# One stationary operand for two neighbouring chunks at all six dyadic levels of an HGRN2 head, the odd chunk's keys and values in reversed order

## The chip, the cores and the metric

The kernel runs on one core of a Trainium2 chip. The metric is the device time of one execution in microseconds (us), the median of several runs. Engines: PE (TensorE, matmuls), DVE (VectorE), ACT (ScalarE), POOL (GpSimd), and SP (SyncE), which issues most of the DMAs.

## What is computed

A decoder layer over 1024 tokens with 16 learned meta tokens ahead of them (D_MODEL 1024, float32): a norm, one input projection, an HGRN2 recurrence of four heads beside a pooling mixer, gates that merge the two, an output projection, and a gated MLP. The change lies in the recurrence:

```python
def _hgrn2_chunk_step(state, xs):
    q, k, v, lf = xs
    b = jnp.cumsum(lf, axis=2)
    o_inter = jnp.einsum('bhtk,bhkv->bhtv', q * jnp.exp(b), state)
    diff = b[:, :, :, None, :] - b[:, :, None, :, :]
    decay = jnp.where(causal, jnp.exp(jnp.where(causal, diff, 0.0)), 0.0)
    scores = jnp.einsum('bhtk,bhtsk,bhsk->bhts', q, decay, k)
    o_intra = jnp.einsum('bhts,bhsv->bhtv', scores, v)
    k_dec = k * jnp.exp(b_last[:, :, None, :] - b)
    new_state = jnp.exp(b_last)[..., None] * state + jnp.einsum('bhsk,bhsv->bhkv', k_dec, v)
    return new_state, o_inter + o_intra
```

The kernel works in chunks of 128 tokens, eight of them and one of the 16 meta tokens. Within a chunk the decay between query t and key s is not a product of one factor of t and one of s that stays in range, so the lower triangle of a chunk is cut into blocks: the pairs within two neighbours (the basic scores, `sb`), and for lv = 2, 4, ... 64 the squares in which the query lies in the second half and the key in the first half of a run of 2 lv tokens. In each such square the decay is taken from the middle of the run, and queries and keys each get a factor of their own.

## The kernel before

Until 250 us the kernel makes norms, the values v, which it stores to DRAM (`vscr`), and the first gates. Then comes the head stage, to about 510 us, and behind it the branch products, the output projection and the MLP. Matrix products are split by hand into a high and a low part (`whi`, `wlo`, `uhi`, `ulo`); the weights' split is a cast on ACT (L140) and a difference on DVE or POOL (L141).

In the head stage the list `ORDER` interleaves projections with the heads: `F` (forget gate, banks `pf`), `Q` (query, `pq`), `G` (output gate, `pg`), `PV` and others are projections, `h0` to `h3` take a head one step further, `c0` to `c3` run a head's logarithms. A list `POOLED` puts single vector operations on POOL; what isn't in it runs on DVE. Within that, the order of ACT's, DVE's and POOL's instructions is set by a scheduler when the program is built, and each engine takes its instructions strictly in that order. The steps of a head:

- `post_f` and `chain_f`: two sigmoids of the forget projection on ACT (f, and 1 - f as kk), three scalings (L600 to L602), two logarithms (L605, L606), their sum on DVE (L607) and the running sum b by a scan of nine parts (L609).
- `level_in`, for the pairs (2, 4), (8, 16), (32, 64): the difference of b to its middle (L643), two exponentials (L646, L647), then the query product (L648) and the key product (L649). Level 64 has no difference but sixteen small exponentials with a bias for each chunk (L640, L641), and a negated middle, `neg` (L638).
- `level_mm`: the matmuls into one bank `sl`. Levels 2 to 16 take a chunk's whole 128 columns of keys and queries as the stationary operand and the 64 queries as the moving one, eight matmuls (L664); what lies outside the squares is not used. Levels 32 and 64 take just the squares, sixteen of 32x32 and eight of 64x64 (L660). Levels 2 to 8 also have a small product of the meta tokens (`sm`, L669).
- `level_out`: a masked copy to the scores `sc` on DVE (L684), or copies on ACT for 32 and 64 (L678).
- then qs and kd, the exponentials of the recurrence (L700, L705), e1 for the basic scores (L715, L716, products L719, L720), transposes of kd (`pt`, copied to kt and ktm at L728 and L732), the basic scores (`sb`, L737, L738), the state products (`ds`, L749, L756) and the outputs (`po`).

The matmuls use eight PSUM banks in turn; one that writes to a bank waits until the engine that empties it is done.

## Time and profile before

| | |
|---|---|
| median of 3 runs | 1367.0 us (1366.5 to 1367.03) |
| profiled execution, span of the core | 1364.2 us, granted PE clock 0.998 |
| PE busy | 1334.8 us (98%) |
| DVE, ACT, POOL busy | 931.3, 601.7, 426.5 us |
| bytes moved by DMA | 236.67 MB, mean 173 GB/s |

The span runs from the first to the last instruction of the core; the median of the runs is 2.8 us above it. In rows of the profile the first two numbers are a start and a duration in us, then engine, line, operation, output tile, input tiles and shapes; "x16" counts instructions in a row, and what stands in brackets is the idle time ahead of it and what ended that. One fp32 matmul shows as two rows. Tile names are printed without their numbers.

### The profile page before, as it was taken

How to read it: one execution, taken by the hardware profiler on the slowest of the kernel's cores; microseconds unless marked ns; L12 is line 12 of the kernel's file. 1: busy time of each engine (PE TensorE's matmuls, PEld its weight loads, DVE VectorE, ACT ScalarE, POOL GpSimd, SP SyncE). 2: the span in 40 equal slices, each digit the busy share in tenths (PEclk: the TensorE clock that was granted, in tenths of full speed). 3: DMA queues.
4: the chain of work that ended last, by engine and by line, in shares of the span. 5: the costliest groups of instructions: out<-in, count | busy, mean ns of one | idle time of the engine just before them, and what ended most of it. 6: DMA issues, size and time to landing. Idle time of an engine off the chain costs nothing. (4 is left out here: it accounts for less than half of the span.)

```text
span 1364.2 us, 20180 instructions
## 1 busy us (share of the span) xinstructions
PE 1334.8 (98%) x7737; PEld 1183.7 (87%) x7737; DVE 931.3 (68%) x1242; ACT 601.7 (44%) x1066; POOL 426.5 (31%) x324
## 2 busy tenths in 40 slices
PE   8999999999989999999999999999999999999997
PEld 7799999999989999987778888888888887888786
DVE  6755644378756557666568888888878777644557
ACT  6543333479766574225655222222322223543343
POOL 2014421227233600051020555454557742000100
PEclk9999999999999999999999999999999999999999
DMA  7134433321110158988876877656677799965534
GB/s 265 48 117 140 124 114 104 101 63 32 49 34 18 34 183 291 323 252 300 286 266 237 230 207 201 193 177 165 158 164 170 181 235 271 380 204 190 183 95 154
DMA packets 141455, 236.67 MB, mean 173 GB/s; under 512 B 9255, under 2 KB 77451, under 8 KB 141359
## 3 DMA queue, kind: packets, MB, share of 16 engines
q1 hardware_dynamic: 129294, 211.00, 46.5%
q0 software_dynamic: 12064, 24.38, 10.5%
q8 instruction: 61, 1.00, 0.3%
q14 instruction: 36, 0.29, 0.1%
HBM read 171.85 MB, written 86.53 MB: 189 GB/s over the span
## 5 line engine op out<-in xcount | busy, mean ns | idle before, releaser
L287 PE MATMUL P<-v,whi 128*128 128x512 f32 (+2 forms) x408 | 142.0, 356 | 3.3 <-ACT p L1501 1.7
L288 PE MATMUL P<-v,whi 128*128 128x512 f32 (+2 forms) x408 | 141.2, 353 | 0.0
L290 PE MATMUL P<-v,wlo 128*128 128x512 f32 (+2 forms) x424 | 135.9, 351 | 0.0
L175 PE MATMUL pd<-rot 128*128 128x512 f32 x272 | 105.9, 390 | 0.3 <-DVE rot L1428 0.3
L176 PE MATMUL pd<-rot 128*128 128x512 f32 x272 | 105.8, 389 | 0.0
L141 POOL TENSOR_TENSOR wlo<-wraw,whi 128x1024 fp32r<-128x1024 f32 (+1 forms) x19 | 45.9, 2416 | 161.9 <-ACT whi L140 86.1
L1428 DVE TENSOR_TENSOR rot<-yt,rot 128x1024 fp32r<-128x1024 f32 x33 | 41.2, 1249 | 72.6 <-ACT rot L1427 72.6
L287 PEld LDWEIGHTS P<-v,whi 128*128 128x128 f32 x408 | 77.2, 189 | 14.5 <-ACT p L1501 2.1
L232 ACT CAST whi<-wraw 128x512 fp32r<-128x512 f32 x78 | 46.1, 618 | 98.0 <-PE P L288 78.8
L288 PEld LDWEIGHTS P<-v,whi 128*128 128x128 f32 x408 | 77.2, 189 | 10.6 <-issue 0.2
L290 PEld LDWEIGHTS P<-v,wlo 128*128 128x128 f32 x424 | 74.3, 189 | 11.4
L233 DVE TENSOR_TENSOR wlo<-wraw,whi 128x512 fp32r<-128x512 f32 x74 | 68.4, 946 | 20.1 <-ACT whi L232 20.1
L1316 POOL TENSOR_TENSOR ys<-y 128x512 f32<-128x512 f32 x22 | 35.3, 1603 | 135.5 <-DVE y L1374 51.5
L1427 ACT CAST rot<-yt 128x1024 fp32r<-128x1024 f32 x33 | 34.6, 1052 | 91.5 <-PE pd L175 91.5
L174 PE MATMUL pd<-rot 128*128 128x512 f32 x272 | 72.6, 390 | 2.1 <-ACT rot L1427 1.2
L258 POOL TENSOR_TENSOR swa<-wraw,wraw 128x512 f32<-128x512 f32 x28 | 44.5, 1591 | 92.9 <-DMA wraw<-in_w_in_dram 56.8
L232 ACT CAST whi<-swa 128x512 fp32r<-128x512 f32 x56 | 33.4, 619 | 86.1 <-PE P L288 77.5
L1360 DVE SCALAR_TENSOR_TENSOR y<-g,par,y 128x1024 f32<-128x1024 f32 x44 | 64.8, 1472 | 0.8
L140 ACT CAST whi<-wraw 128x1024 fp32r<-128x1024 f32 (+1 forms) x28 | 26.4, 942 | 85.4 <-PE ppv L188 17.2
L174 PEld LDWEIGHTS pd<-rot 128*128 128x128 f32 x272 | 51.0, 188 | 13.4 <-ACT rot L1427 1.6
L232 ACT CAST whi<-swb 128x512 fp32r<-128x512 f32 x56 | 33.4, 618 | 63.1 <-PE P L288 59.3
L175 PEld LDWEIGHTS pd<-rot 128*128 128x128 f32 x272 | 51.1, 188 | 11.3 <-DVE rot L1428 0.7
(391 smaller groups left out, 4191.2 us busy)
## 6 DMA issues: line engine op xcount, KB each, us to landing
wraw<-in_w_in_dram SPq DMA_DIRECT2D x36, 512.0 KB
yt<-ysum SPq DMA_DIRECT2D x33, 512.0 KB
wraw<-in_ffn_w_gate_dram SPq DMA_DIRECT2D x26, 512.0 KB
wraw<-in_w_out_dram SPq DMA_DIRECT2D x24, 512.0 KB
wraw<-in_ffn_w_up_dram SPq DMA_DIRECT2D x22, 512.0 KB
wsum<-in_ffn_w_down_dram SPq DMA_DIRECT2D x22, 512.0 KB
ysum<-ys SPq DMA_DIRECT2D x11, 768.0 KB
sa<-sscr SPq DMA_DIRECT2D x16, 513.0 KB
```

The costliest lines, as they stand in the source:

```text
L141: eng.tensor_tensor(lo, raw, rr(hi), ALU.subtract)
L174: pe.matmul(ps, ahi, bhi, start=first, stop=False)
L175: pe.matmul(ps, ahi, blo, start=False, stop=False)
L176: pe.matmul(ps, alo, bhi, start=False, stop=last)
L232: act.copy(hi, src)
L233: (pool_e if 4 <= i < 2 * self.early else dve).tensor_tensor(lo, src, rr(hi), ALU.subtract)
L258: pool_e.tensor_tensor(s1, a21, a22, ALU.add)
L287: pe.matmul(d, whi[:, k, :], xh[:, c : c + w], start=(k == 0 and onto is None), stop=False, **go)
L288: pe.matmul(d, whi[:, k, :], xl[:, c : c + w], start=False, stop=False, **go)
L290: pe.matmul(x[:, o : o + w], wlo[:, k, :], xh[:, c : c + w], start=False, stop=(k == 3), **go)
L1360: dve.scalar_tensor_tensor(a, g[:, j : j + SEQ], cvw[:, j, m : m + 1], a, ALU.mult, ALU.add)
L1428: dve.tensor_tensor(lo, src, rr(hi), ALU.subtract)
```

## The change

Two neighbouring chunks now have one stationary operand. Of each chunk only the keys of first halves are used at a level, 64 of 128 columns. The odd chunk's keys are stored in reversed order, and then its first halves fall, seen from the chunk's end, on the columns that the even chunk leaves free. So the key products of an even and an odd chunk are written into the two halves of one 128-column operand in a new tile `dk`, and one matmul multiplies it with the 128 queries of both chunks. A level takes four matmuls of 128x128 instead of eight, and levels 32 and 64 have the same form.

What goes with it: the second sigmoid is written to b, and kk is scaled from there in three pieces, the odd chunks' reversed (L613, L615); every key product is done in two halves, with a piece of its own for the meta tokens on levels 2 to 8 (L666, L670); e1's key product in three (L737, L741); the copies of levels 32 and 64 to sc become six per head instead of three (L693); kd's exponentials of odd chunks write reversed (L721). The masks become twice as wide, and those of 32 and 64 go. The values of odd chunks are needed reversed as well: four DMAs copy a stored chunk from DRAM to DRAM in reversed order (L516), each behind the store of that chunk on SP, and each head loads its values by two DMAs instead of one. The program has 7211 matmul instructions for 7339, 945 DVE tensor_tensor instructions for 909, 36 ACT table loads for 32, and 386 ACT activations for 378.

The core of the diff:

```diff
-            nc.sync.dma_start(vd[(t0 - NM) // P], v)
+            c = (t0 - NM) // P
+            nc.sync.dma_start(vd[c % 2, c // 2], v)
+            if c % 2:
+                there, here = (vd[i, c // 2].rearrange("t (j v) -> j t v", j=2) for i in (2, 1))
+                nc.sync.dma_start(there, here[:, ::-1])
...
-            act.activation(kk[:, lo : lo + n], ps[:, :n], AF.Sigmoid, scale=-1.0)
+            act.activation(b[:, lo : lo + n], ps[:, :n], AF.Sigmoid, scale=-1.0)
...
-        act.activation(kk, kk, AF.Copy, scale=oml[:, hh])
+        act.activation(kk[:, :NM], b[:, :NM], AF.Copy, scale=oml[:, hh])
+        for z in range(2):
+            act.activation(parity(kk, z), time_order(b, z), AF.Copy, scale=oml[:, hh])
...
+    def parity(t, z):
+        return t[:, NM:L].rearrange("p (c z t) -> p c z t", z=2, t=P)[:, :, z, :]
+
+    def time_order(t, z):
+        return parity(t, z)[:, :, ::-1] if z else parity(t, z)
...
-            eng(f"lk{lv}.{h}").tensor_tensor(db[:, :, 0, :], db[:, :, 0, :], blocks(kk, lo, lv)[:, :, 0, :], ALU.mult)
-            return d
-
-        def level_mm(lv, qk):
+            e = eng(f"lk{lv}.{h}")
+            if lo == 0:
+                dm, km = (t[:, :NM].rearrange("p (b two h) -> p b two h", two=2, h=lv)[:, :, 0, :] for t in (d, kk))
+                e.tensor_tensor(dm, dm, km, ALU.mult)
+            for z in range(2):
+                o_, a, b_ = (t.rearrange("p c (b two h) -> p c b two h", two=2, h=lv)[:, :, :, z, :]
+                             for t in (dk.rearrange("p (c t) -> p c t", t=P), time_order(d, z), parity(kk, z)))
+                e.tensor_tensor(o_, a, b_, ALU.mult)
+            return d, dk
+
+        def level_mm(lv, qk, dk):
             ps = bank("sl")
-            half = lv >= 32
-            for c in range(NCH):
-                t = NM + c * P
-                if half:
-                    for i in range(P // (2 * lv)):
-                        s, n = t + 2 * lv * i, 2 * lv * i
-                        pe.matmul(ps[n : n + lv, c * lv : (c + 1) * lv], qk[:, s : s + lv], qk[:, s + lv : s + 2 * lv],
-                                  start=True, stop=True)
-                    continue
-                rhs = qk[:, t : t + P].rearrange("p (b two h) -> p b two h", two=2, h=lv)[:, :, 1, :]
-                pe.matmul(ps[:, c * 64 : (c + 1) * 64], qk[:, t : t + P], rhs, start=True, stop=True)
+            for c in range(NCH // 2):
+                t = NM + 2 * c * P
+                rhs = qk[:, t : t + 2 * P].rearrange("p (b two h) -> p b two h", two=2, h=lv)[:, :, 1, :]
+                pe.matmul(ps[:, c * P : (c + 1) * P], dk[:, c * P : (c + 1) * P], rhs, start=True, stop=True)
...
-                o3 = sc.rearrange("p (c t) -> p c t", c=NCH)
-                p3 = ps[:, : NCH * lv].rearrange("p (c h) -> p c h", c=NCH)
+                o4 = sc.rearrange("p (c z t) -> p c z t", z=2, t=P)
+                p4 = ps.rearrange("p (c z t) -> p c z t", z=2, t=P // 2)
                 for i in range(P // (2 * lv)):
-                    n = 2 * lv * i
-                    act.copy(o3[n : n + lv, :, n + lv : n + 2 * lv], p3[n : n + lv])
+                    q0 = 2 * lv * i + lv
+                    for z, n in ((0, 2 * lv * i), (1, P - 2 * lv * i - lv)):
+                        act.copy(o4[n : n + lv, :, z, q0 : q0 + lv], p4[n : n + lv, :, z, lv * i : lv * (i + 1)])
...
-                act.activation(kc[:, c], bc[:, c], AF.Exp, bias=bc[:, c, w - 1 : w], scale=-1.0)
+                kt_ = kc[:, c, ::-1] if t0 and c % 2 else kc[:, c]
+                act.activation(kt_, bc[:, c], AF.Exp, bias=bc[:, c, w - 1 : w], scale=-1.0)
...
-        k2 = kk.rearrange("p (b two) -> p b two", two=2)[:, :, 1]
         eng(f"e1q.{h}").tensor_tensor(q2, q2, e1[:, : L // 2], ALU.mult)
-        eng(f"e1k.{h}").tensor_tensor(k2, k2, e1[:, L // 2 :], ALU.mult)
+        ek = e1[:, L // 2 :]
+        km = kk[:, :NM].rearrange("p (b two) -> p b two", two=2)[:, :, 1]
+        eng(f"e1k.{h}").tensor_tensor(km, km, ek[:, : NM // 2], ALU.mult)
+        ek = ek[:, NM // 2 :].rearrange("p (c z t) -> p c z t", z=2, t=P // 2)
+        for z in range(2):
+            k2 = parity(kk, z).rearrange("p c (b two) -> p c b two", two=2)[:, :, :, 1 - z]
+            eng(f"e1k.{h}").tensor_tensor(k2, k2, ek[:, :, z, ::-1] if z else ek[:, :, z], ALU.mult)
```

Lines move by 11 to 21: what was L605 and L606 is L618 and L619, L609 is L622, L638 L652, L643 L657, L646 to L649 are L660 to L670, L664 and L660 are L678, L678 is L693, L700 L715, L705 L721, L715 L731, L797 L818.

On PE the sequence is the same but for the level groups. The products of head 1's levels 2 and 4 and head 0's levels 32 and 64, before:

```order
L664 MATMUL sl_3149<-d_3046 128x64 x8
L669 MATMUL sm_3158<-d_3046 16x8
L664 MATMUL sl_3160<-d_3052 128x64 x8
L669 MATMUL sm_3169<-d_3052 16x8
L660 MATMUL sl_3204<-d_3013 32x32 x16
L660 MATMUL sl_3221<-d_3019 64x64 x8
```

The same place on PE, changed:

```order
L678 MATMUL sl_3156<-d_3049,dk_3048 128x128 x4
L683 MATMUL sm_3161<-d_3049 16x8
L678 MATMUL sl_3163<-d_3057,dk_3048 128x128 x4
L683 MATMUL sm_3168<-d_3057 16x8
L678 MATMUL sl_3209<-d_3012,dk_3011 128x128 x4
L678 MATMUL sl_3214<-d_3019,dk_3011 128x128 x4
```

Eight matmuls are four, and sixteen and eight small ones are four each.

POOL, at head 0's levels 32 and 64 (d_3013 and d_3019 before, d_3012 and d_3019 changed) and head 1's levels 4 and 8 (d_3052 and d_3175; d_3057 and d_3175), before:

```order
L643 TENSOR_TENSOR d_3052<-b_2841 128x1040
L648 TENSOR_TENSOR d_3013<-d_3013,q_2737 128x16x32
L648 TENSOR_TENSOR d_3019<-d_3019,q_2737 128x8x64
L649 TENSOR_TENSOR d_3019<-d_3019,kk_2629 128x8x64
L649 TENSOR_TENSOR d_3052<-d_3052,kk_2840 128x130x4
L643 TENSOR_TENSOR d_3175<-b_2841 128x1040
L141 TENSOR_TENSOR wlo_3136<-wraw_3133,whi_3135 128x1024
```

POOL at the same place, changed:

```order
L662 TENSOR_TENSOR d_3012<-d_3012,q_2739 128x16x32
L640 MEMSET sc_3044 128x1024
L670 TENSOR_TENSOR dk_3011<-d_3019,kk_2629 128x4x64
L662 TENSOR_TENSOR d_3019<-d_3019,q_2739 128x8x64
L670 TENSOR_TENSOR dk_3011<-d_3019,kk_2629 128x4x64
L657 TENSOR_TENSOR d_3057<-b_2849 128x1040
L657 TENSOR_TENSOR d_3175<-b_2849 128x1040
L666 TENSOR_TENSOR d_3057<-d_3057,kk_2848 128x2x4
L670 TENSOR_TENSOR dk_3048<-d_3057,kk_2848 128x64x4 x2
```

Before, the difference of head 1's level 4 (L643, d_3052) stands ahead of head 0's products; changed (L657, d_3057), it stands behind head 0's level-64 products.

ACT, at the two logarithms of head 2 (f_406, then f_3141; changed f_410, then f_3148), before:

```order
L605 ACT_TABLE_LOAD
L605 ACTIVATE f_406_3142<-f_406_3142 128x1040
L606 ACTIVATE f_3141<-f_3141 128x1040
L700 ACT_TABLE_LOAD
L700 ACTIVATE qs_3233<-b_2630 128x1040
L705 ACTIVATE kd_3234<-b_2630 128x16
L705 ACTIVATE kd_3234<-b_2630 128x128 x8
L715 ACTIVATE e_418_3249<-f_2631 128x520
L716 ACTIVATE e_418_3249<-f_2631 128x520
```

ACT at the second logarithm, changed:

```order
L618 ACT_TABLE_LOAD
L618 ACTIVATE f_410_3149<-f_410_3149 128x1040
L693 COPY sc_2746<-sl_3209 32x4x32 x2
L693 COPY sc_2746<-sl_3214 64x4x64 x2
L721 ACT_TABLE_LOAD
L721 ACTIVATE kd_3226<-b_2630 128x128
L723 COPY ebl_3237<-qs_3225 128x8
L731 ACTIVATE e_423_3241<-f_2631 128x520
L732 ACTIVATE e_423_3241<-f_2631 128x520
L619 ACT_TABLE_LOAD
L619 ACTIVATE f_3148<-f_3148 128x1040
L140 CAST whi_3325<-wraw_3323 128x1024
```

Before, the two logarithms stand together and head 0's qs, kd and e1 behind them. Changed, the copies, the last kd and e1 stand between the two, with a table load on each side; qs and the other kd stand further ahead, before the first logarithm.

More of the change, by code (lines that the diff above doesn't have):

```diff
@@ L541, in v_feat @@
                 dve.tensor_copy(um[:, :, NM:], rr(ulo[:, :, :NM]))
-    vd = dram.tile([NCH, P, 512], F32, name="vscr")
+    vd = dram.tile([3, NCH // 2, P, 512], F32, name="vscr")
     vmeta = const.tile([P, 512], F32, name="vmeta")
@@ L548, in trunk_kernel, with mask_of @@
     vm_hl, vm_low = vm_[:, :512], vm_[:, 512:]
-    LEVELS = (2, 4, 8, 16, 32, 64)
+    MASKED = (2, 4, 8, 16)
     masks = {}
-    mbase = const.tile([P, P], U8, name="mbase")
-    mtmps = slot(P + len(LEVELS) * P // 2, name="mtmps")
-    mtmp = mtmps[:, :P]
-    pool_e.memset(mtmp, 1.0)
-    pool_e.affine_select(out=mtmp, in_=mtmp, compare_op=ALU.is_ge, fill=0.0, base=0,
-                         pattern=[[-2, P // 2], [0, 2]], channel_multiplier=1)
-    pool_e.affine_select(out=mtmp, in_=mtmp, compare_op=ALU.is_ge, fill=0.0, base=0,
-                         pattern=[[2, P // 2], [1, 2]], channel_multiplier=-1)
-    pool_e.tensor_copy(mbase, mtmp)
-    for i, h in enumerate(LEVELS):
-        mt = mtmps[:, P + i * P // 2 : P + (i + 1) * P // 2]
-        pool_e.memset(mt, 1.0)
-        pool_e.affine_select(out=mt, in_=mt, compare_op=ALU.is_ge, fill=0.0, base=0,
-                             pattern=[[-2 * h, P // (2 * h)], [0, h]], channel_multiplier=1)
-        pool_e.affine_select(out=mt, in_=mt, compare_op=ALU.is_ge, fill=0.0, base=h - 1,
-                             pattern=[[2 * h, P // (2 * h)], [0, h]], channel_multiplier=-1)
-        masks[h] = const.tile([P, P // 2], U8, name=f"mask{h}")
-        pool_e.tensor_copy(masks[h], mt)
+    mbase = const.tile([P, 2 * P], U8, name="mbase")
+    mtmps = slot((2 + len(MASKED)) * P, name="mtmps")
+    pool_e.memset(mtmps, 1.0)
+    def mask_of(dst, mt, low, high):
+        n = mt.shape[1] // 2
+        for z, (cm, at) in enumerate(((1, 0), (-1, P - 1))):
+            for (base, pattern), sign in ((low, 1), (high, -1)):
+                m = mt[:, z * n : (z + 1) * n]
+                pool_e.affine_select(out=m, in_=m, compare_op=ALU.is_ge, fill=0.0, base=base + sign * at,
+                                     pattern=pattern, channel_multiplier=sign * cm)
+        pool_e.tensor_copy(dst, mt)
+    mask_of(mbase, mtmps[:, : 2 * P], (0, [[-2, P // 2], [0, 2]]), (0, [[2, P // 2], [1, 2]]))
+    for i, h in enumerate(MASKED):
+        masks[h] = const.tile([P, P], U8, name=f"mask{h}")
+        mask_of(masks[h], mtmps[:, (2 + i) * P : (3 + i) * P], (0, [[-2 * h, P // (2 * h)], [0, h]]),
+                (h - 1, [[2 * h, P // (2 * h)], [0, h]]))
     def V(c, h):
@@ L627, in head_steps, with level_in @@
         pool_e.memset(scm, 0.0)
[L630 removed]
+        def level_in(lv, dk):
             lo = 0 if 2 * lv <= NM else NM
```

24 lines of the change are left out of this document (12 added, 12 removed).

## The prediction

> **What bounds the kernel now.** I read the busy totals, the stages in windows, PE's waits, and then what stands ahead of each group of level products. The profiled execution's span is 1364.2 us and the median of the runs 1367.0, so the sum is made on 1364.2 and 2.8 is added at the end.
>
> ```profile
> span 1364.2 us, 20180 instructions
> PE 1334.8 (98%) x7737; PEld 1183.7 (87%) x7737; DVE 931.3 (68%) x1242; ACT 601.7 (44%) x1066; POOL 426.5 (31%) x324
> ...
> 310.00:360.00 50.00, 49.90 (x430) 48.49 (x429) 46.61 (x47) 45.38 (x93) 30.47 (x15) 1.00 0.16 45
> ...
> PE ds L749 <- ACT ktm L732: 3.6, 1, 3.6
> PE sl L664 <- DVE d L649: 0.7, 1, 0.7
> ```
>
> The columns of a window are its length, then busy time of PE, PE's weight loads, DVE, ACT and POOL. PE runs without a gap and sets the end; in the head stage it waits 3.6 + 0.7 us in all. But from 310 to 360 DVE is busy 46.61 of 50 us and ACT 45.38: there PE is only just fed. Time taken from PE is a gain only where the work that feeds it can come earlier too.
>
> **What PE saves.**
>
> ```profile
> L664 PE MATMUL sl<-d x256: 217/275/326, 280.7 to 435.8; 128*128 128x64 f32 x128
> L737 PE MATMUL sb<-q,kk x64: 275/275/275, 345.3 to 474.1; 128*128 128x128 f32 x64
> ...
> 311.81 1.89 PE L664 MATMUL sl<-d 128*128 128x64 f32 x16
> 313.77 2.00 PE L664 MATMUL sl<-d 128*128 128x64 f32 x16
> ...
> 315.76 1.75 PE L660 MATMUL sl<-d 128*32 128x32 f32 x47
> 317.44 0.42 PE L187 MATMUL pq<-uhi,whi 128*128 128x348 f32 x1
> 345.31 1.95 PE L737 MATMUL sb<-q,kk 128*128 128x128 f32 x16
> 353.20 0.48 PE L749 MATMUL ds<-vmeta,ktm 16*128 16x128 f32 x2
> ```
>
> One fp32 matmul is two rows. A level 2 to 16 has 16 rows of 64 moving columns, 1.89 us with the last row's tail, 0.12 a row. The basic scores (sb) have the same stationary 128x128 with 128 moving columns: 16 rows in 1.95 us, again 0.12. So twice the moving columns cost nothing and four matmuls for eight save 0.9 us a group: 16 groups, 14.4 us. Levels 32 and 64 had 48 rows of small tiles, 317.44 - 315.76 = 1.7 us; 16 full rows are 1.85: +0.1 for each head. PE's work falls by 14.0 us.
>
> The Trainium skill, TensorE: Matmul & The Clock Gate (Back-to-back issue gap), lets the gap grow with the moving columns, some 60 cycles up to 64 and 134 at 128; by that the halved count would save nothing, and the sum would lack the 14.4. The two rows above differ from it here; they agree with the same page's weight-load section (columns / 1.2, 107 ns for 128).
>
> **What the feeding engines pay.** Small edits first.
>
> ```profile
> 344.94 0.69 DVE L649 TENSOR_TENSOR d<-d,kk 128x520 f32<-128x520 f32 x1
> ...
> POOL 2014421227233600051020555454557742000100
> ```
>
> ACT: the key's scale in three pieces instead of one (L613, L615: +0.3 a head), six score copies for three (L693). DVE and POOL: each key product (L670) in two halves of 256 and, on levels 2 to 8, a piece of the meta tokens: 0.4 + 0.4 + 0.15 by elements for DVE's 0.69, about +0.3 each; on POOL similar. No row shows a reversed read or write. Its price lies between none and the instruction's time once more; I take none, because the products of L648 and L649, which step over elements, cost no more than plain ones (0.69 for 520). The masks are built in POOL's first slice of 34 us (busy two tenths, the next slice 0) for a use at 280: their extra selects cost nothing. The four reversed copies of v:
>
> ```profile
> 62.18 0.47 SPq L512 DMA_DIRECT2D vscr<-v  x1
> ...
> 68.04 0.39 SPq L239 DMA_DIRECT2D wraw<-in_w_in_dram  x1
> 79.08 0.32 SPq L799 DMA_DIRECT2D gscr<-sg  x1
> ```
>
> Each waits on SP until a store has landed. Behind the third copy stand two loads of gate weights (68.04 is the second), behind the fourth none until after 79.08. No row shows how long that store takes; even 5 us more on the load at 68.04 leave it ahead of SP's next use by 6. I take nothing; if that cover is gone, those few us come once, ahead of the gates.
>
> The rest follows from the order, which has the same PE sequence but other ACT, DVE and POOL sequences.
>
> **Place one, head 1, levels 2 and 4.**
>
> ```profile
> 299.33 0.21 ACT L638 ACTIVATE neg<-b 128x8 f32<-128x8 f32 x1 [4.06 <-DVE b L609]
> 300.84 1.28 ACT L640 ACT_TABLE_LOAD   x1
> ...
> 307.22 0.34 ACT L640 ACTIVATE d<-b,neg 128x64 f32<-128x64 f32 x1
> 307.46 0.34 ACT L641 ACTIVATE d<-b 128x64 f32<-128x64 f32 x1
> 299.37 5.10 POOL L643 TENSOR_TENSOR d<-b 128x1040 f32<-128x1040 f32 x1 [10.10 <-DVE b L609]
> 306.17 1.29 POOL L648 TENSOR_TENSOR d<-d,q 128x512 f32<-128x512 f32 x1 [1.69 <-ACT d L646]
> 309.12 3.46 POOL L649 TENSOR_TENSOR d<-d,kk 128x512 f32<-128x512 f32 x2
> 311.35 1.79 DVE L648 TENSOR_TENSOR d<-d,q 128x520 f32<-128x520 f32 x1
> 331.73 1.92 POOL L643 TENSOR_TENSOR d<-b 128x1040 f32<-128x1040 f32 x1 [6.61 <-issue]
> ```
>
> Before, POOL makes level 4's difference (L643, 299.37) as soon as head 1's scan is done; the products end at 312.6 (POOL) and 313.14 (DVE) for the matmul at 313.77: 0.6 us of slack, while PE would now arrive 3.6 us earlier. In the changed order that difference stands behind head 0's level-64 products, which need the sixteen exponentials. By rows: scan 299.3, table load (1.28) to 300.8, level 32's two exponentials 1.1 (332.39 below has one of that size), sixteen at 0.24 (the last two rows' spacing) 3.9: about 305.8. Then POOL: product halves and query product 2.6, difference 1.92, level 8's difference 1.92, level 4's key pieces 1.4: 7.8 us, 313.6 with POOL alone. Beside DVE two products took 3.46 where 2 x 1.29 would do, 1.34 times: 316.3. I take the middle, 315.0, because DVE has work for only part of it; the group 0.95, levels 32 and 64 1.85, the small ones 0.1: PE is through at 317.9, against 317.44 before. All that is saved up to here (six groups, 5.4) goes into waits: +0.5 (bounds -0.9 and +1.8).
>
> **Place two, head 2, around 345.**
>
> ```profile
> 326.51 1.06 ACT L606 ACTIVATE f<-f 128x1040 f32<-128x1040 f32 x1
> 327.58 1.28 ACT L700 ACT_TABLE_LOAD   x1
> 328.88 1.07 ACT L700 ACTIVATE qs<-b 128x1040 f32<-128x1040 f32 x1
> 329.85 2.63 ACT L705 ACTIVATE kd<-b 128x16 f32<-128x16 f32 x9
> 332.39 0.66 ACT L715 ACTIVATE e<-f 128x520 f32<-128x520 f32 x1
> 328.87 2.72 DVE L609 TENSOR_TENSOR_SCAN b<-f 128x16 f32<-128x16 f32 x9
> 387.90 6.43 DVE L609 TENSOR_TENSOR_SCAN b<-f 128x16 f32<-128x16 f32 x9
> 387.65 2.42 POOL L141 TENSOR_TENSOR wlo<-wraw,whi 128x1024 fp32r<-128x1024 f32 x1 [6.48 <-PE pt L730]
> 313.07 3.05 DVE L643 TENSOR_TENSOR d<-b 128x1024 f32<-128x1024 f32 x1
> 346.42 1.15 ACT L797 ACTIVATE sg<-pg 128x342 f32<-128x342 f32 x3
> ```
>
> Before, ACT does both logarithms of head 2 (the second, L606, ends 327.57) and then head 0's exponentials. In the changed order qs, kd, e1 (1.0 + 2.6 + 1.1), two more table loads (2 x 1.28, one on each side of them) and the longer copies and scales (0.6) come ahead of the second logarithm: +7.9, it ends at 335.5. DVE adds (1.24), makes q's product (0.69 free, 2.2 beside POOL) and scans. The scan takes 2.72 alone and 6.43 where POOL works beside it. POOL has e1k, a difference, L141 (2.4), a query and a key product and a memset in its queue, some 9 us without a gap, so the second is the nearer row: scan done at 345.4 (bound with free DVE 340.2), 331.6 before. ACT's neg waits for it, and behind neg stand head 1's sixteen exponentials (3.9), level 2's (1.1), L140 (1.0), a table load and the gate's three copies (1.0): +8.4, and these copies free the banks that PE's next small products need. Level 4's exponentials, which stood ahead of the gate copies before, now need another load: its products come at 345.4 + 11.8, its group 1 us later, so L749 starts at 358.2 where it was 353.20 (+5.0). If its difference on DVE runs beside L141 as at 313.07 (3.05 for 1.23) there are 1.8 more. I take them, since L141 is issued just then: +6.9, in which the saving of ten groups is gone (bounds: -0.2 with the scan at 340.2 and no such lock, and +6.9).
>
> The Trainium skill, SBUF — State Buffer (Who interferes with whom) says that a DVE instruction with two SBUF inputs and a GpSimd instruction that reads SBUF exclude one another, the second blocking fully; the scan's two rows, 2.72 and 6.43, agree. By its other statement, that one which only writes excludes nothing, the memset at the queue's end would not count, and the scan would end 0.9 earlier.
>
> **Place three, head 3's scan.**
>
> ```profile
> 385.53 1.06 ACT L606 ACTIVATE f<-f 128x1040 f32<-128x1040 f32 x1
> ...
> 394.77 0.48 PE L749 MATMUL ds<-vmeta,ktm 16*128 16x128 f32 x2 [3.63 <-ACT ktm L732]
> 395.25 2.43 PE L756 MATMUL ds<-vh,kt 128*128 128x128 f32 x14
> ```
>
> Before, PE waits for ktm behind neg, and the query projection begins at 395.25 + 2.43 = 397.7. Changed, head 3's sigmoids are split by exponentials (two more loads, 2.6), so its second logarithm, done at 386.6, comes 6.9 + 2.6 later; the sum and the scan, again beside L141, take the 7.8 they took (to 394.3 before), 403.8, and the projection needs a bank that DVE empties 0.7 behind that: 404.5, +6.8. Without a lock in places two and three (scan in 2.72, place two at -0.2) ACT and DVE are done by 393.5, and PE, two groups ahead, comes at -2.
>
> **Sum.** Levels 2 and 4 of head 3 end in a wait for DVE already (the 0.7 above): one of their savings is lost. The other three groups give -2.7 and split products cost +0.3. Of these 2.7 the last head's state products, which PE reaches earlier than their feeders, can take back 0 to all; I say 1, as for a wait like the 0.7. 6.8 - 2.7 + 0.3 + 1 = +5.4 on 1364.2: 1369.6, or 1372.4 on the median's scale. The bounds: -2 - 2.7 + 0.3 = -4.4 (1362.6), and 6.8 + 2.4 (one more POOL instruction of 2.42 in place three's scan) + 0.3 = +9.5 (1376.5). Reversed operands at twice the time would add 1.8 on ACT ahead of place two's logarithm (four kd of 0.3, half a scale 0.6) and 0.4 at each of eight groups that wait: +5.
>
> **Rivals.** A: head 2's scan is not held up. From a scan end before about 341 place two gives under +1, place three is PE's own time, and the kernel is faster: 1362.6 (1353.0 if place one feeds PE as well, 14 off). The 2.72 scan beside an idle POOL speaks for it, POOL's full queue against. B: the waits eat just the gain, scan end near 343, place two at +2.6: 2.6 - 2.7 + 0.3 + 1 = +1.2, 1368.2. C: PE is paid by moving columns, so that 8 rows of 128 take the 1.89 of 16 rows of 64. PE saves nothing, but in places one to three it waits anyway, so only the last 2.7 are lost: 1375. The sb rows speak against it. (The page on TensorE above has such a rule.) D: reversed operands cost double: 1377.4; no row speaks for or against.
>
> **How the numbers follow.** A change of 0.2% (2.7 us) is about what a measurement of this kernel can tell from none: faster is under 1364.3, slower above 1369.7. My forecast, waits larger than the gain by a few us, 0.57; A 0.16; B 0.15; C 0.03; D 0.09. So faster 0.16, same 0.15, slower 0.69. The predicted time is 1372.5, the likeliest case's own range 1369.7 to 1376.5; the whole, leaving out A's lower part and D with the upper bounds, 1363 to 1382.
>
> **What the profile would show.** Level groups of 8 rows in about 0.95 us; 36 ACT table loads for 32; PE idle before sl near 308 to 314 (released by POOL or DVE key products) and near 346 to 357 (released by sg, then by level 4's product); head 2's scan spread over more than 5 us; the second logarithm of head 2 at about 335. I am wrong if PE's waits in the head stage sum to less than 14 us, if a group takes 1.8 us, or if an engine's instruction with a reversed operand is longer than its twin.

## The result, and the profile after

| | before | after |
|---|---|---|
| median (lowest to highest) | 1366.75 us (1365.7 to 1367.03, 4 runs) | 1375.76 us (1374.47 to 1376.95, 4 runs) |
| span of the profiled execution | 1364.2 us | 1375.2 us (its time 1376.95) |
| PE busy, granted clock | 1334.8 us, 0.998 | 1330.7 us, 0.989 |

The changed kernel is slower by 9.0 us; the ratio is 1.0069, 95% interval 1.0054 to 1.0083. The forecast was 1372.5, slower by 5.4 in its sum, with a range of 1363 to 1382. The direction and the places were right; the size was short by 3.3 us. One experiment below, e7, has two executions of eleven, at 1627 and 3377 us, that stand far off the rest; its median is 1366.5 us with them and 1366.0 without.

The page of the changed kernel:

```profile
span 1375.2 us, 19757 instructions
PE 1330.7 (97%) x7481; PEld 1178.0 (86%) x7481; DVE 926.9 (67%) x1278; ACT 611.5 (44%) x1090; POOL 429.0 (31%) x330
```

Its head stage in windows of 50 us (length, then busy time of PE, weight loads, DVE, ACT and POOL, then the granted clock):

```profile
310.00:360.00 50.00, 37.53 (x239) 36.36 (x240) 31.55 (x43) 41.24 (x79) 28.95 (x20) 0.88 0.11 34
360.00:410.00 50.00, 47.28 (x318) 45.73 (x318) 35.43 (x56) 43.83 (x97) 15.90 (x8) 0.95 0.11 34
```

Two things stand here. From 310 to 360 PE, which was busy for 49.90 of 50 us, is busy for 37.53: it waits. And the clock column, which read 1.00, reads 0.88. PE's busy time fell by 4.1 us, not by the 14.0 of the forecast, because part of what is left runs at a lower clock: in windows of 1 us, busy time times the missing share of the clock comes to 1.7 us before and 11.4 after (8.0 in the head stage, the rest at 662 to 666 and 706 to 710), and 14.0 less 9.7 is 4.3. PE's waits in the head stage (in total, times, longest):

```profile
PE sl L678 <- DVE dk L670: 5.9, 2, 3.2
PE sm L763 <- ACT sg L818: 4.6, 1, 4.6
PE sl L678 <- POOL dk L670: 2.5, 1, 2.5
PE pq L187 <- DVE sc L759: 2.5, 1, 2.5
PE pg L187 <- ACT q L629: 2.4, 1, 2.4
```

With two of 1.0 and 0.7 for head 2's states they add to 19.6 us, where before there were 4.3. PE's rows at places one, two and three, which answer to 311.81, 313.77, 353.20 and 397.34 of before:

```profile
312.73 1.15 PE L678 MATMUL sl<-d,dk 128*128 128x128 f32 x8 [3.16 <-DVE dk L670]
316.53 2.08 PE L678 MATMUL sl<-d,dk 128*128 128x128 f32 x8 [2.52 <-POOL dk L670]
...
356.57 0.24 PE L763 MATMUL sm<-q,kk 128*16 128x16 f32 x2 [4.64 <-ACT sg L818]
357.01 5.14 PE L678 MATMUL sl<-d,dk 128*128 128x128 f32 x24 [0.20 <-ACT sg L818]
362.21 1.16 PE L678 MATMUL sl<-d,dk 128*128 128x128 f32 x8
363.44 0.48 PE L770 MATMUL ds<-vmeta,ktm 16*128 16x128 f32 x2
...
404.77 0.42 PE L187 MATMUL pq<-uhi,whi 128*128 128x348 f32 x1 [2.50 <-DVE sc L759]
```

Read the durations of one form against each other. Eight rows of 128x128 take 1.15 or 1.16 at 312.73 and 362.21, and 2.08 at 316.53, behind a second wait; twenty-four take 5.14, not three times 1.16. It is the same instruction at another clock. The granted clock in short windows of the changed kernel (same columns), and then the one such place of the kernel before:

```profile
316.00:318.00 2.00, 1.47 (x7) 1.47 (x8) 0.26 (x2) 1.98 (x7) 2.00 (x2) 0.50 0.00 0
318.00:320.00 2.00, 2.00 (x11) 1.75 (x11) 0.75 (x2) 1.99 (x3) 0.80 (x2) 0.50 0.02 6
320.00:322.00 2.00, 2.00 (x16) 2.00 (x15) 1.46 (x4) 2.00 (x4) 1.26 (x1) 0.83 0.85 254
...
355.00:360.00 5.00, 3.23 (x16) 3.15 (x17) 2.58 (x4) 4.96 (x8) 3.34 (x1) 0.50 0.05 15
360.00:365.00 5.00, 5.00 (x36) 4.58 (x36) 4.90 (x9) 5.00 (x15) 0.00 (x0) 0.83 0.00 0
405.00:410.00 5.00, 5.00 (x23) 5.00 (x23) 5.00 (x4) 2.70 (x10) 4.29 (x2) 0.66 0.00 0
425.00:430.00 5.00, 4.11 (x15) 2.94 (x16) 4.45 (x12) 2.55 (x5) 0.93 (x1) 0.66 0.00 0
```

```profile
396.00:400.00 4.00, 4.00 (x20) 4.00 (x19) 0.73 (x1) 3.99 (x10) 0.00 (x0) 0.57 0.43 135
```

Behind four of its waits PE runs for 3 to 5 us at half of the clock; the values between 0.50 and 1.00 are of windows in which it changes (from 406 to 409 alone the column reads 0.50). Busy time times the missing share gives what that costs: 0.7 + 1.0 + 0.3 at 316 to 322, 1.6 + 0.9 at 355 to 365, 1.7 and 1.4 at the last two, 7.6 us together. Before it was 4.00 x 0.43 = 1.7, once, behind the wait of 3.63 us. These 5.9 us stand in no term of the forecast.

### The profile page after: what moved, and what is told of

Its sections match the earlier page's. It is cut to its first block, busy times and chain, and to the rows that moved or that the text cites. A ratio compares the mean times of both kernels' runs of the same rounds, so it can differ in the third digit from the quotient of the medians.

```text
span 1375.2 us, 19757 instructions
## 1 busy us (share of the span) xinstructions
PE 1330.7 (97%) x7481; PEld 1178.0 (86%) x7481; DVE 926.9 (67%) x1278; ACT 611.5 (44%) x1090; POOL 429.0 (31%) x330
## 3 DMA queue, kind: packets, MB, share of 16 engines
q0 software_dynamic: 12064, 24.38, 10.2%
## 5 line engine op out<-in xcount | busy, mean ns | idle before, releaser
L288 PEld LDWEIGHTS P<-v,whi 128*128 128x128 f32 x408 | 77.3, 189 | 10.6 <-issue 0.2
L175 PE MATMUL pm<-wlo,zc 128*114 128x512 f32 x144 | 58.3, 405 | 3.9 <-DMA wlo<-wlos 3.9
```

Of the source, the lines that this page charges most:

```text
L175: pe.matmul(ps, ahi, blo, start=False, stop=False)
L288: pe.matmul(d, whi[:, k, :], xl[:, c : c + w], start=False, stop=False, **go)
```

## The experiments

Each ran beside the kernel before on the same chip. "After" is the changed kernel, 1375.8 us and ratio 1.0069; e1, e4 and e11 start from the kernel before, all others from after.

### e1: the PE part alone

Levels 2 to 16 of the kernel before take four matmuls of 128 moving columns, and nothing else changes; the odd chunks' keys are left out, so their scores of these levels are not the right ones:

```diff
-                rhs = qk[:, t : t + P].rearrange("p (b two h) -> p b two h", two=2, h=lv)[:, :, 1, :]
-                pe.matmul(ps[:, c * 64 : (c + 1) * 64], qk[:, t : t + P], rhs, start=True, stop=True)
+                if c % 2:
+                    continue
+                rhs = qk[:, t : t + 2 * P].rearrange("p (b two h) -> p b two h", two=2, h=lv)[:, :, 1, :]
+                pe.matmul(ps[:, c * 64 : (c + 2) * 64], qk[:, t : t + P], rhs, start=True, stop=True)
```

> The kernel before with PE's part alone: levels 2 to 16 take four matmuls of 128x128 over two chunks with the even chunk's columns as the stationary operand; no reversed order, no extra work elsewhere (the odd chunks' scores of these levels are not computed rightly). PE's work falls by 14.4 us. Theory (the gain is only what the feeding engines let through): head 1's levels 2 and 4 wait 4 to 6 us, the clock then sinks for some us, head 3 waits more: 1359 to 1364, about 1361. Rival (PE is the bound, what ate the gain is the added work on ACT, DVE and POOL): 1352 to 1354.

Measured: 1358.55 us, ratio 0.9948 (0.9932 to 0.9963), 8.0 us faster than the kernel before of its batch and half a us under the theory's range. Of the 14.4 forecast for PE 8.0 arrive; the rest goes mainly into new waits and the clock behind them. The waits are not where the theory had them: head 1's levels 2 and 4 wait 1.7 us, not 4 to 6. The longest is at head 1's state products. It, and the window in which place two lies:

```profile
PE ds L758 <- DVE sc L740: 3.5, 1, 3.5
```

```profile
300.00:360.00 60.00, 56.52 (x445) 54.35 (x444) 57.37 (x63) 51.34 (x111) 41.38 (x18) 0.97 0.16 46
```

PE is no longer full there, and DVE is busy for 57.37 of 60 us. So halving the matmuls is a gain as such, and moving columns are not what PE is paid by (rival C). It is worth 8, not 14, with the queues of the kernel before.

### e2: PE's saving given back

After, with each matmul of levels 2 to 16 issued twice:

```diff
-                pe.matmul(ps[:, c * P : (c + 1) * P], dk[:, c * P : (c + 1) * P], rhs, start=True, stop=True)
+                for _ in range(2 if lv < 32 else 1):
+                    pe.matmul(ps[:, c * P : (c + 1) * P], dk[:, c * P : (c + 1) * P], rhs, start=True, stop=True)
```

> The changed kernel with each level matmul of levels 2 to 16 issued twice, so that PE's work is as before and the added work and order of the other engines remain. Theory (places one to three are set by ACT, DVE and POOL, and PE's saving is lost in waits): PE waits 10 to 14 us less than the changed kernel's 20, and the time is 1374 to 1379, hardly above the changed kernel's 1375.8. Rival (PE's saving did arrive and the added work costs its own time on top): 14 us above the changed kernel, 1388 to 1390.

Measured: 1374.76 us, ratio 1.0063 (1.0048 to 1.0079). The time is the theory's; PE's waits in the head stage fall from 19.6 to 11.2 us, by 8 and not by 10 to 14. Fourteen us of PE work more change nothing: with the order that after has, ACT, DVE and POOL set the pace, and a lighter PE waits for them.

### e3: idle matmuls in place one's waits

Twelve matmuls of constants ahead of head 1's level 2 and nine ahead of level 4:

```diff
             ps = bank("sl")
+            junk(ps, {(1, 2): 12, (1, 4): 9}.get((h, lv), 0))
             for c in range(NCH // 2):
```

> The changed kernel with 12 and 9 idle 128x128 matmuls ahead of head 1's levels 2 and 4, where PE waits 3.2 and 2.5 us. Theory (a wait of PE lowers the granted clock for about 6 us after it): with PE kept busy the granted clock stays at 1.0 there, the eight rows of level 4 take 1.1 us instead of 2.08, the sixteen of levels 32 and 64 take 2.0 instead of 3.00, and the query projection starts about 2 us earlier; the whole gains 1 to 2.5 us since place two is set by other engines. Rival (the rows are slow because of their operands or the bank): the same 2.08 and 3.00 and the same time within 0.5 us.

Measured: 1372.35 us, ratio 1.0040 (1.0028 to 1.0053), 3.4 us under after by the medians, more than the 1 to 2.5 expected. PE's rows at place one:

```profile
308.72 2.84 PE L634 MATMUL sl<-ident,onesm 128*128 128x128 f32 x24
311.93 1.17 PE L683 MATMUL sl<-d,dk 128*128 128x128 f32 x8 [0.37 <-DVE dk L674]
...
315.83 1.16 PE L683 MATMUL sl<-d,dk 128*128 128x128 f32 x8 [0.38 <-POOL dk L674]
...
318.86 0.41 PE L187 MATMUL pq<-uhi,whi 128*128 128x348 f32 x1
```

The products arrive no earlier: level 4's group starts at 315.83, 0.7 ahead of 316.53, and these 0.7 stood already at the first level product (281.26 for 281.95). But the groups behind it run at full clock, and from level 4's start to the query projection it is 3.03 us for after's 4.91. Work that is thrown away gains 1.9 us at this place, and that is the clock. That these 1.9 are in the 3.4 is not shown: head 2's second logarithm ends 0.8 earlier, hardly more than the 0.7, and the scheduler moved a part of kd on ACT and, on DVE, head 0's product of q with its exponential (L734), which in after stands between head 2's sum and its scan; so this scan begins at 339.58 for 341.67.

### e4: the DMAs alone

The kernel before with the four reversed copies of v and two loads of v per head; the reversed copies are made but not used:

```diff
-            nc.sync.dma_start(vd[(t0 - NM) // P], v)
+            c = (t0 - NM) // P
+            nc.sync.dma_start(vd[c % 2, c // 2], v)
+            if c % 2:
+                there, here = (vd[i, c // 2].rearrange("t (j v) -> j t v", j=2) for i in (2, 1))
+                nc.sync.dma_start(there, here[:, ::-1])
```

> The kernel before with the four reversed copies of v from DRAM to DRAM and two loads of v per head, nothing else (the copies are not used). In the changed kernel the first level product starts at 281.95 instead of 280.75, 1.2 us late, ahead of everything else that was changed. Theory A: the copies on SP and the loads behind them cause it: first level product 1.0 to 1.4 us late, time 1368. Theory B, as predicted: the copies cost nothing, the 1.2 us are another execution's scatter: first level product at 280.7, time 1366.8.

Measured: 1366.25 us, ratio 0.9996 (0.9984 to 1.0007): theory B's time. But the first level product starts at 281.50, 0.75 us late. A load of gate weights behind the third copy lands later (ACT's cast of it starts at 74.02 for 69.83), and at 90 us PE waits for the gates (before, e4, after):

```profile
PE P L287 <- ACT sg L797: 0.2, 1, 0.2
PE P L287 <- ACT sg L802: 0.9, 1, 0.9
PE P L287 <- ACT sg L818: 1.5, 1, 1.5
```

In the ten traces of kernels with the copies this wait is 0.6 to 1.5 us, in the three without them 0.2. So the copies do delay the gates, by less than e4's median can show; in the profiled execution of after it is the 1.2 us by which the level products begin late.

### e5, e6, e7: place one and place two undone

e5 writes head 1's step ahead of head 0's, so that level 4's difference stands on POOL ahead of head 0's products again:

```diff
-ORDER = ("F0 c0 Q0 h0 F1 h0 c1 Q1 h0 h1 F2 h1 c2 ...
+ORDER = ("F0 c0 Q0 h0 F1 h0 c1 Q1 h1 h0 F2 h1 c2 ...
```

> The changed kernel with one step of the order exchanged: head 1's part of the queues is written out ahead of head 0's (Q1 h1 h0 in place of Q1 h0 h1), so that level 4's difference of head 1 stands on POOL ahead of head 0's level-64 products, as in the kernel before. Theory (place one's two waits of 3.2 and 2.5 us and the low clock behind them, 2.6 to 3.4 us, come from that queue position): PE no longer waits ahead of head 1's levels 2 and 4, but head 0's levels 32 and 64 now wait for their products, some 3 us; net 0 to 4 us under the changed kernel's 1375.8, that is 1371.5 to 1375. Place two stays as it is (second logarithm at about 337). Rival (place one's waits are covered by place two's wait, which ends by ACT's own sequence whatever PE has lost before): gate copies and ds at the same time as in the changed kernel, the whole within 1 us of it, 1375 to 1377.

Measured: 1372.79 us, ratio 1.0050 (1.0038 to 1.0062). PE passes head 1's levels at 309.02 and 310.15 without a wait, and waits for head 0's level 64 instead, before the first of these rows:

```profile
315.94 1.50 PE L678 MATMUL sl<-d,dk 128*128 128x128 f32 x8 [3.27 <-POOL dk L670]
317.09 0.64 PE L187 MATMUL pq<-uhi,whi 128*128 128x348 f32 x1
...
352.46 0.24 PE L763 MATMUL sm<-q,kk 128*16 128x16 f32 x2 [5.40 <-ACT sg L818]
```

The query projection starts 4.4 us earlier than in after, the gate's products 4.1 earlier, and 3.0 reach the end. The rival's prices (within 1 us) are out; the second logarithm, at 336.24 for after's 336.97, stayed, and place two's wait grew from 4.64 to 5.40.

e6 issues head 0's qs, kd, ebl and e1 on ACT behind head 2's second logarithm, as before:

```diff
-        act.activation(f, f, AF.Ln)
+        heads[h]["ln"] = act.activation(f, f, AF.Ln)
...
+        ln_ = heads[{0: 2}[h]]["ln"].ins if h in {0: 2} else None
+        hold = tc.issue_after(ln_) if ln_ is not None else __import__('contextlib').nullcontext()
+        hold.__enter__()
         act.activation(qs, b, AF.Exp)
...
+        hold.__exit__(None, None, None)
```

> The changed kernel with head 0's exponentials qs, kd, ebl and e1 issued on ACT behind head 2's second logarithm, as in the kernel before; everything else in its place. Theory (place two's 10 us come from ACT's sequence, with 1.3 + 1.3 us of table loads and 4.7 us of exponentials ahead of the second logarithm, and from the scan beside POOL): the logarithm ends near 331, the scan 5 to 6 us earlier, the wait of the gate's small products falls from 4.6 to under 1 us and ds starts 4 to 6 us earlier; the low clock after it goes too: 1368 to 1372. Rival (the scan is held up by POOL's queue alone, whatever its start, and ends near 347 again): ds within 1.5 us of 363.4 and the whole within 1.5 us of the changed kernel, 1374 to 1377.

Measured: 1371.76 us, ratio 1.0052 (1.0037 to 1.0066). The time is in the theory's range, its steps only partly so. The two logarithms stand together, and the scan takes 2.72, as in the kernel before, and is done at 334.06, 14.6 us earlier than in after and not 5 to 6. But the gate's wait fell to 3.1, not under 1, and ds came at 360.75, 2.7 earlier:

```profile
331.34 2.72 DVE L622 TENSOR_TENSOR_SCAN b<-f 128x16 f32<-128x16 f32 x9
...
349.32 0.68 ACT L660 ACTIVATE d<-d 128x520 f32<-128x520 f32 x1 [3.01 <-POOL d L657]
```

With the scan out of the way, ACT waits 3.01 us for a difference that POOL makes behind a query product, a key product and a memset. The next late thing was POOL's queue.

e7 takes both edits and three instructions of head 1's level 32 off POOL's list:

```diff
-POOLED = ("... lk32.1 ... lq32.1 ... sub32.1 ...").split()
+POOLED = ("...").split()
```

> Both of these edits, and three instructions of head 1 (level 32's query and key products and its difference) made on DVE in place of POOL, so that POOL has 3 to 4 us less to do around head 2's scan. Theory (waits in places one and two, and their low clock, are all that keeps the saving of 14 us from showing): 1361 to 1367, faster than the kernel before. Rival (the feeding engines are full whatever their order, and work taken from one place comes back as a wait in the next): 1368 to 1373.

Measured: 1366.46 us, ratio 0.9991 (0.9978 to 1.0003). The gate copies come at 348.42, 7.6 us before after's, and its wait is 1.4:

```profile
348.93 0.21 PE L765 MATMUL sm<-q,kk 128*16 128x16 f32 x2 [1.42 <-ACT sg L820]
349.28 2.96 PE L676 MATMUL sl<-d,dk 128*128 128x128 f32 x24
```

The 24 rows that took 5.14 us in after take 2.96 here, at full clock. The three edits together give 9.3 us, what the change had lost; the time is at the upper end of the theory's range. Waits of 3.3 us for POOL, and of 2.7 and 2.5 us for DVE, are left. The first is place one again, now at head 0's level 64, the others are behind place two; that they keep the rest of the 14 from showing is argued here and tried in e9 and e10.

### e8: idle matmuls at five waits

As e3, and more of them: sixteen ahead of the second half of head 1's basic scores, nine ahead of head 3's state products and nine ahead of head 3's level 4.

```diff
+            junk(ps, {(1, 2): 12, (1, 4): 9, (3, 4): 9}.get((h, lv), 0))
...
+                junk(ps, {1: 16}.get(h, 0))
...
+                junk(ps, {3: 9}.get(h, 0))
```

> The changed kernel with idle matmuls (128x128 of constants) issued into PE's five longest waits of the head stage: 12 and 9 ahead of head 1's levels 2 and 4, 16 ahead of the second half of head 1's basic scores, 9 ahead of head 3's state products and 9 ahead of head 3's level 4. They compute nothing that is used and bring no product earlier. Theory (behind each wait PE runs for 4 to 6 us at half its granted clock, and that low clock, not the wait, is what the prediction's sum lacked): granted clock near 1.00 through 306 to 430, and the time falls by 6 to 9 us, to 1367 to 1370, beside 3.4 us for place one alone. Rival (the low clock is covered by the next wait, which ends by ACT's and DVE's own sequence): the gate's and head 3's products start no earlier than in the changed kernel, and the time stays at 1371 to 1375.

Measured: 1373.57 us, ratio 1.0052 (1.0038 to 1.0065): the theory's 1367 to 1370 is missed, the rival's 1371 to 1375 holds. Two reasons show. Two of the five fills stand in the wrong place: the basic scores at place two are head 0's, head 1's come at 394, where PE did not wait, and there the sixteen cost 3.74 us; and the state products ahead of the wait at 404 are head 1's, head 3's come at 498, where the nine cost 2.17 (second and third row below). And the time won at place one came back as a longer wait for ACT at the gate's projection (4.16 for 2.4 us) with a low clock of its own behind it:

```profile
338.66 0.66 PE L187 MATMUL pg<-uhi,whi 128*128 128x342 f32 x1 [4.16 <-ACT q L629]
...
395.08 3.74 PE L634 MATMUL sb<-ident,onesm 128*128 128x128 f32 x32
...
498.88 2.17 PE L634 MATMUL ds<-ident,onesm 128*128 128x128 f32 x18
```

```profile
324.00:340.00 16.00, 11.84 (x76) 11.41 (x75) 7.97 (x8) 15.78 (x28) 6.40 (x6) 0.91 0.11 34
340.00:350.00 10.00, 10.00 (x54) 10.00 (x54) 7.75 (x13) 5.42 (x19) 7.57 (x6) 0.80 0.18 52
```

ACT is busy 15.78 of 16 us in the first of the two windows: there it is the bound. So what the clock gives back at place one does not reach the end where ACT's sequence ends last behind it, and there the rival is right. What the low clock at the other places is worth to the whole, e8 does not show, since two of its fills missed them.

### e9, e10, e11: the queues set anew

If the waits are a matter of order, an order should exist in which they are gone. e9 and e10 keep the changed kernel's PE work and arithmetic and change only the order: e5's exchange, e6's place for the exponentials, and another list of POOL's instructions. e10's list, with neg behind level 32's exponentials:

```diff
-ORDER = ("... Q1 h0 h1 F2 ... PV1 h3 sp0 PV2 h2 h3 sa1 sp1 sp2 PP0 h2 PV3 ...
+ORDER = ("... Q1 h1 h0 F2 ... PV1 sp0 h3 PV2 h2 sa1 h3 PP0 h2 sp2 sp1 PV3 ...
...
+POOLED = ("e1k.3 e1q.1 e1q.2 e1q.3 kdmul.1 kdmul.2 kdmul.3 kdsub.2 lk16.3 lk2.0 lk2.2 lk32.2 lk4.1 lk64.0 lk64.2 "
+          "lk8.0 lk8.1 lk8.2 lk8.3 lq16.3 lq32.2 lq32.3 lq4.0 lq64.0 lq64.2 lq64.3 lq8.0 osg.2 qsmul.2 qsmul.3 "
+          "sub2.0 sub2.3 sub32.0 sub32.2 sub4.1 sub4.3 sub8.0 sub8.1 sub8.3 wBA2 wBA6 wBA7 wBB2 wF0 wF1 wF2 wF3 wPP2 "
+          "wPV0 wPV3 wQ0").split()
```

> The changed kernel with the queues set anew around the same PE work: head 1's steps ahead of head 0's as in e5, head 0's exponentials behind head 2's second logarithm as in e6, the three scaled copies of the key gate behind the logarithms, and another list of instructions for POOL (the logarithms' sum of head 3 and level 4's products there, level 32's on DVE). Theory (the saving of 14 us is real, and what hid it are waits of ACT's, DVE's and POOL's order and the low clock behind them): no wait of PE above 3 us, the low clock gone, 1354 to 1361, faster than the kernel before and no slower than the PE part alone (1358.6). Rival (the three feeding engines are full in this stage, so that a wait shifted from one place comes back at the next, as in e8): 1364 to 1368, like e7's 1366.5.

> The same with another list: more of the key products and differences of heads 1 to 3 on POOL, the key gate's copies ahead of the logarithms as in the changed kernel, and neg behind level 32's exponentials. Theory: 1356 to 1363. Rival as above: 1364 to 1368.

Measured: e9 1357.70 us, ratio 0.9935 (0.9917 to 0.9953); e10 1356.46 us, ratio 0.9926 (0.9912 to 0.9940). Both theories hold in their times and waits; the low clock is not wholly gone (0.97 in e10's window below, 0.50 from 349 to 351). e10 is faster than after by 19.3 us and than the kernel before by 10.5 of its batch. Its page, the window of places one and two, and its longest waits in the head stage:

```profile
PE 1321.5 (98%) x7481; PEld 1170.2 (86%) x7481; DVE 916.8 (68%) x1257; ACT 608.0 (45%) x1088; POOL 450.2 (33%) x351
```

```profile
310.00:360.00 50.00, 44.90 (x304) 43.04 (x303) 35.94 (x57) 48.66 (x107) 21.88 (x17) 0.97 0.15 44
```

```profile
PE sl L680 <- DVE dk L672: 4.4, 3, 2.8
```

PE's busy time is 13.3 us under the kernel before's, against 14.0 forecast (the low clock costs 1.7 us in the head stage of either), and no wait of the head stage is above 2.8. POOL is busy 21 us longer than in after, DVE 10 us less.

e11 is the control: the kernel before with e10's edits of the queues and without the shared operand.

> The kernel before with the same edits of the queues as in e10 and nothing else. Theory (e10's gain comes from the shared operand; the kernel before waits for 4.3 us in this stage, so other queues can give it no more than these and the low clock behind the one long wait, 1.7): 1362 to 1372, PE busy as before, near 1335 us. Rival (the new queues are better for any kernel, and the shared operand still gives nothing): near e10, 1356 to 1360.

Measured: 1369.44 us, ratio 1.0021 (1.0011 to 1.0031). The queues alone gain nothing. Between e10 and e11 only the change itself differs: 1.0021 - 0.9926 = 0.95% of 1366, 13 us. A part of these is that the order of e10 suits the old work worse than its own order; with each kernel in its own order the gain is 10.5. PE's busy time is 1345.4 us and not near 1335, but the profiled execution of e11 is the slowest of its twelve (1375.66 us), and its head stage loses 10.0 us to the low clock.

## Why the prediction was right, and where it was short

**PE's saving: right, a little large.** A group of eight rows takes 1.16 us with its tail for 2.00 of sixteen before, 24 rows 2.96 where nothing slows them, and in e10 PE's busy time falls by 13.3. Rival C is out by these rows and by e1, and with it the Trainium skill's rule in TensorE: Matmul & The Clock Gate (Back-to-back issue gap) as applied there to these fp32 matmuls. The Trainium skill gives those gaps there for a matmul by itself, and says that in a stream of weight loads and matmuls both set the pace.

**Small edits and reversed operands: right; the DMAs not quite.** Reversed operands cost nothing (rival D): kd's exponentials of even and odd chunks start 0.29 to 0.30 us apart throughout, and of two key products of 256 at one level, one of them with a reversed operand, one takes 0.43 us and the other 0.42.

```profile
323.88 2.34 ACT L721 ACTIVATE kd<-b 128x16 f32<-128x16 f32 x8
...
352.25 0.43 DVE L670 TENSOR_TENSOR dk<-d,kk 128x256 f32<-128x256 f32 x1 [2.18 <-ACT d L655]
...
353.20 0.42 DVE L670 TENSOR_TENSOR dk<-d,kk 128x256 f32<-128x256 f32 x1
```

Eight in 2.34 is 0.29 each, as nine in 2.63 before. The copies of v were put at nothing and delay the gates by 1.2 us in the profiled execution (e4); the forecast had named that place.

**Place one: right in kind, +0.5 forecast, +4.0 measured** (the query projection at 321.44 for 317.44). The forecast let head 1's scan end at 299.3, as before; it ends at 300.87, and 1.2 of that are the late gates. ACT's first row behind the scan, and the last of POOL's queue:

```profile
300.90 0.22 ACT L652 ACTIVATE neg<-b 128x8 f32<-128x8 f32 x1 [2.09 <-DVE b L622]
...
315.06 1.41 POOL L670 TENSOR_TENSOR dk<-d,kk 128x256 f32<-128x256 f32 x2
```

POOL is done at 316.47, 15.6 us behind the scan; the forecast's 315.0, the middle between its bounds, is 15.7 behind. So the middle was right and the start was not, which is 1.5 of the miss. The other 2.0 are clock: from 316.53 to the projection it is 4.91 us, for 2.9 in the forecast.

**Place two: right in kind, +6.9 forecast, +10.2 measured** (L770 at 363.44, L749 at 353.20). The chain in after, ACT and DVE:

```profile
336.97 1.07 ACT L619 ACTIVATE f<-f 128x1040 f32<-128x1040 f32 x1
...
341.67 6.96 DVE L622 TENSOR_TENSOR_SCAN b<-f 128x16 f32<-128x16 f32 x9
...
348.66 0.22 ACT L652 ACTIVATE neg<-b 128x8 f32<-128x8 f32 x1 [6.04 <-DVE b L622]
...
356.06 1.15 ACT L818 ACTIVATE sg<-pg 128x342 f32<-128x342 f32 x3
```

The logarithm ends at 338.0 for 335.5: +2.5, of which 1.2 is again the late start. The sum and the scan took 10.6 for 9.9, the scan itself 6.96 beside POOL, near the 6.43 of the row chosen; rivals A and B are out, and with 6.96 beside POOL and 2.72 without it (e6) the Trainium skill's SBUF — State Buffer (Who interferes with whom) agrees. It agrees on the memset too, which only writes: beside it (347.03 to 347.98) the scan's parts start 0.3 us apart, as without POOL. From neg to ds it is 14.8, where the forecast had 14.6 with the lock. But the 1.8 for that lock on level 4's difference did not occur (L657 took 1.24 at 354.89); in part the clock came in its stead: the 24 rows took 5.14 for 2.96 in e7, and level 4's group starts at 362.21, 0.9 behind its last key product. A right sum with a wrong term in it.

**Place three: +6.8 forecast, +7.4 measured** (404.77 for 397.34 by the starts; the forecast's own 404.5 is missed by 0.3). The number is right by luck. Head 3's second logarithm ends at 396.35, forecast 386.6 + 6.9 + 2.6 = 396.1, but place two was 3.3 later than the 6.9, and the 2.6 for two more table loads did not come. ACT waits there for PE's forget projection, the two added loads (368.80 and 370.93) run ahead of that wait, and from its end to the logarithm it is 19.4 us, where it was 19.8 before:

```profile
376.91 1.05 ACT L140 CAST whi<-wraw 128x1024 fp32r<-128x1024 f32 x1 [3.54 <-PE pf L188]
...
395.30 1.05 ACT L619 ACTIVATE f<-f 128x1040 f32<-128x1040 f32 x1
```

What follows was right: the sum and the scan, beside POOL again (6.43), and the projection 8.4 us behind the logarithm.

**Behind it: a gain of 1.4 forecast (-2.7 + 0.3 + 1), 2.9 lost by the rows.** The last head's outputs start at 502.92 for 492.60, +10.3. (The medians differ by 9.0; the profiled execution is the slowest of its four.) Most of this lies between 404.77 and 430.26. Head 3's level 4 waits 2.73 us, 2.0 more than before, where the forecast let one group's saving of 0.9 go. And the waits of 2.50 and 2.73 us each have a low clock behind them, 1.7 and 1.4 us, about 2 us more than before lost behind this place. The waits for head 2's states, 1.0 and 0.7, are near the 1 us assumed, though not at the last head's state products, which do not wait.

So these terms failed: the copies, put at nothing (1.2 us in this execution); the second logarithm of place two (1.3 beyond that); two table loads that cost nothing (2.6, the other way); and a wait of PE, priced at its own length, where the clock behind it costs some 2 us at place one, 1 at place two and 2 behind place three. The row that shows this price stood in the profile of before, at 396 to 400, and had been quoted without its clock (2.43 us for 14 rows, against 1.83 at 353.61 of the same kernel). The whole 5.9 us of clock would have been too much, since what is lost ahead of ACT's next wait need not reach the end (e3, e8).

The Trainium skill, TensorE: Matmul & The Clock Gate (Part 1: The HAM clock gate), says that the array falls to half clock after an idle window of some 3.4 us and returns after about as long of busy time, in windows that run freely. This case's trace agrees on the half clock (0.50) and on a stretch of 3 to 5 us. On the threshold it does not: of waits from 2.1 to 2.8 us, those ahead of 405 and 426 in after are followed by 0.50, the one of 2.8 in e10 at 411 by 1.00; and in e4 a wait of 0.74 (ahead of 417.5) is followed by 0.50 from 420 to 422, where the same wait of the kernel before (ahead of 416.8) is followed by 1.00.

## What to carry to other kernels

A wait of the matmul engine can cost more than its length, by the slower clock behind it. Look for that price in the profile of before, in two rows of one form with different durations behind and without a wait, and ask whether another engine ends last behind it. When a change takes work from the engine that sets the end, the gain is only as large as what the feeding engines can advance. An order of their queues that suits the old work need not suit the new, and another has to be tried before the change is judged: here the same change costs 9 us with one order and gains 10.5 with another. A control with the new order and the old work (e11) tells the two apart.

## What was not expected of the hardware

- Idle matmuls in a wait, which bring nothing forward, made a place 1.9 us faster (e3).
- A wait of 2.5 us can be followed by 3.4 us at half of the clock (after, 406 to 409.4), and one of 2.8 by none (e10, 411). One and the same wait of 0.74 us was followed by half clock in e4 and by full clock in the kernel before. In e11 the clock is 0.50 from 418 to 431, behind one wait of 2.8, the dearest such place seen. What decides between them, no run here settles.
- One scan of nine parts takes 2.72 us, 4.27 (e5) or 6.96 (after), by what POOL does at the time.
